# Differential attention with the values stationary, and its norm by a block matrix, in a one-layer hybrid decoder

## The chip, the cores and the metric

One core of a Trainium2 chip runs the whole layer as one program. Its engines work side by side, each through a list of instructions in order, and wait for each other by semaphores: TensorE (PE: matrix products, with PEld its weight loads), VectorE (DVE), ScalarE (ACT), GpSimd (POOL) and SyncE (SP, which starts DMAs here). The metric is the device time of one execution in microseconds.

## The reference

One layer on x of 256 x 1024: a SwiGLU, a mixer and another SwiGLU, each followed by a layer norm. The mixer runs three causal attentions of six heads with 64 columns each, and merges them with sigmoid gates:

```python
x = layer_norm(alpha*x + 0.5*swiglu(x, ...))
h = x @ w_in                      # q, k, v of the three branches, and gates
# MoBA: one block of 256 here, so causal softmax attention with ALiBi
# differential attention, per head:
p = softmax(s, axis=-1)           # s: two score maps, 32 columns each
w = p[:, :, 0] - lam * p[:, :, 1]
o = w @ v
o = o * rsqrt(mean(square(o), axis=-1) + 1e-5) * subln_g * (1 - lambda_init)
# stick-breaking attention: weights by sums of log-sigmoids
merged = sum(sigmoid(g_b + c_b) * (o_b @ w_br_b) for b in branches)
x = layer_norm(alpha*x + merged @ w_out)
x = layer_norm(alpha*x + 0.5*swiglu(x, ...))
```

## The kernel before

All products are exact to nearly float32: a weight chunk and an activation are each split into a high and a low part in float32r (`act_split`: ACT writes the high part, DVE the rest), and three products are summed. `Weights` streams chunks of 128 x 1024 through nine buffers; L106 (ACT) and L107 (DVE) are its split, L109 and L110 the same for the chunks that carry the sublayer norm's gain.

The order of all work is written out by the program while it is built. `MIX` lists the projections of q and k (`project`, which ends with L826 to L830: DVE and ACT take q and k out of their two banks), the gates (`gates`, whose banks are taken out by L868) and the branch products (`branch`, L890). `Pe` counts a modelled time as products are written, and pieces that were put off with `pe.later(delay, fn)` are written between two products once that model reaches their time. Each engine then works through what was written for it in just that order.

The heads go in pairs, first three stick-breaking ones, then three differential, then three MoBA. A pair passes through stages, one per slot, and a slot begins at the earliest 10 us (`PACE`) behind the one before, by the model. In a slot every pair under way takes its next stage, sorted by `KINDS`. A differential pair has four: `scores` (the products of q and k, then maxima on DVE in L616, exponentials on ACT in L622, and `combine`), `turn` (transposes of the weights, copied out as eT in L630), `pv` (values, then the norm), `turn_o` (transposes of o, split into oT). A MoBA pair has `scores` (with L616 and L622 too, and `norm` put off by 2 us: a reciprocal in L665 and four scalings in L668), `turn` and `valT`. The products with weights use four PSUM banks (`acc`), the attention four others (`att`); a bank is written again only after its readers are through, the oldest free one first.

```python
KINDS = ("sums", "turn_o", "pv", "turn", "valT", "scores")
def project(b, p):
    ...
    at = max(pe.t + 1.0, next_start[0])
    next_start[0] = at + PACE
    ...
    pe.later(at - pe.t, lambda: slot(attend[b](p, *res)))
```

Of the kernel before, what the change touches and what calls it, by code (L numbers as in the profile page):

```python
# [10 lines left out]
F32 = mybir.dt.float32  # L11
F32R = mybir.dt.float32r
AF = mybir.ActivationFunctionType
ALU = mybir.AluOpType
PSUM = bass.MemoryType.PSUM

P = 128
S = 256
# [4 lines left out]
HD = 64  # L23
BW = 384
NP = BW // P
EPS = 1e-5
# [27 lines left out]
T_M = 3.4  # L54
N_T = 4.5
M_N = 2.0
D_S = 2.5
E_BUFS = 6


class Weights:
# [129 lines left out]
def trunk(ctx: ExitStack, tc: tile.TileContext, start_d, x_d, ln_g, ln_b, gu_d, gun_d, down_d, v_d, qk_d, gate_d,  # L191
          b_gate, lam_d, subln_d, br_d, wo_d, out_d):
    nc = tc.nc
# [8 lines left out]
    small = ctx.enter_context(tc.tile_pool(name="small", bufs=4))  # L202
    acc = ctx.enter_context(tc.tile_pool(name="acc", bufs=4, space=PSUM))
    att = ctx.enter_context(tc.tile_pool(name="att", bufs=4, space=PSUM))
# [25 lines left out]
    pe = Pe(nc)  # L230
# [4 lines left out]
    def act_split(dst_h, dst_l, src):  # L235
        nc.scalar.activation(dst_h, src, AF.Copy)  # L236
        nc.vector.tensor_tensor(dst_l, src, dst_h.bitcast(F32), op=ALU.subtract)


    with ExitStack() as es:  # L240
        st = es.enter_context(tc.tile_pool(name="start", bufs=1))
        raws = []
        for k in range(KT):
            r = st.tile([P, S + 512], F32, name=f"sraw{k}")
# [12 lines left out]
        ident = const.tile([P, P], F32, name="ident")  # L257
        make_identity(nc, ident)
        first = []
        for k in range(KT):  # L260
# [3 lines left out]
            c = slice((k % 2) * 512, (k % 2) * 512 + 512)  # L264
# [19 lines left out]
    with ExitStack() as es:  # L284
        st = es.enter_context(tc.tile_pool(name="start2", bufs=1))
        mhalf = const.tile([P, 8], F32, name="mhalf")
# [37 lines left out]
    nlam = const.tile([P, 1], F32, name="nlam")  # L324
# [231 lines left out]
    with ExitStack() as es:  # L556
        mp = es.enter_context(tc.tile_pool(name="mp", bufs=1))
        qkp = es.enter_context(tc.tile_pool(name="qkp", bufs=3))
        ep = es.enter_context(tc.tile_pool(name="ep", bufs=E_BUFS))
        V = mp.tile([P, 2, 3 * BW], F32, name="V")  # L560
        oT = [mp.tile([P, NP, 2 * S], F32R, name=f"oT{b}") for b in range(3)]
# [26 lines left out]
        def vcol(b, h):  # L588
            return slice(b * BW + h * HD, b * BW + (h + 1) * HD)

        def scores(maps, qT, kT, row_q):


            st, mv = (qT, kT) if row_q else (kT, qT)
            for kind in range(2):
                for r0, n, ps in maps:
                    r, tp = slice(r0, r0 + n), (r0, 0)
                    if row_q and kind == 0:
                        out, a, b_ = ps[:, 0:P], slice(0, P), slice(0, P)
                    elif row_q:  # L600
                        out, a, b_ = ps[:, P:BW], slice(P, S), slice(0, S)
                    elif kind == 0:
                        out, a, b_ = ps[:, 0:S], slice(0, P), slice(0, S)
                    else:
                        out, a, b_ = ps[:, S:BW], slice(P, S), slice(P, S)
                    pe.mm(out, st[r, a], mv[r, b_], row_q or kind == 0, row_q, tile_position=tp, share=len(maps),
                          skip_group_check=not row_q)
# [3 lines left out]
        def exp_rows(maps):  # L611


            for ps, slope, e, nmx, _ in maps:
                for t, cs in enumerate(TILES):
                    nc.vector.tensor_tensor_reduce(e[:, cs], ps[:, cs], base[:, cs], -slope, 3e38, ALU.add, ALU.min,  # L616
                                                   accum_out=nmx[:, t:t + 1])
            W.quiet = False
            W.pump()
            for _, _, e, nmx, sm in maps:  # L620
                for t, cs in enumerate(TILES):
                    nc.scalar.activation(e[:, cs], e[:, cs], AF.Exp, bias=nmx[:, t:t + 1], scale=-1.0,  # L622
                                         accum_out=sm[:, t:t + 1])
# [9 lines left out]
        def values_T(b, p, eTs):  # L633

            po = att.tile([P, 512], F32, name="att")
            for kt, cs, ws in ((0, slice(0, S), slice(0, S)), (1, slice(P, S), slice(S, BW))):
                for r in range(2):
                    pe.mm(po[r * HD:(r + 1) * HD, cs], V[:, kt, vcol(b, 2 * p + r)], eTs[r][:, ws], kt == 0, kt == 1,
                          tile_position=(0, r * 64), share=2, skip_group_check=True)
            act_split(oT[b][:, p, 0:S], oT[b][:, p, S:2 * S], po[:, 0:S])  # L640
            pairs_done[b] += 1

        exps = [0]
        pairs_done = [0, 0, 0]
# [1 line left out]

        KINDS = ("sums", "turn_o", "pv", "turn", "valT", "scores")

        def moba_pair(p, qT, kT):
            sm = small.tile([P, 2, 2], F32, name="sm")
# [23 lines left out]
        def diff_pair(p, qT, kT):  # L676
            sm = small.tile([P, 2, 2, 2], F32, name="smd")
            nmx = small.tile([P, 2, 2, 2], F32, name="nmxd")
            ee, eTs, os_ = [], [], []

            def start():
                banks = [(acc if i < 2 else att).tile([P, 512], F32, name="acc" if i < 2 else "att")
                         for i in range(4)]
                scores([(i * 32, 32, banks[i]) for i in range(4)], qT, kT, True)
                ee.extend(ep.tile([P, BW], F32, name="e") for _ in range(4))
                exp_rows([(banks[i], SLOPES[2 * (2 * p + i // 2) + 1], ee[i], nmx[:, i % 2, i // 2, :],
                           sm[:, i % 2, i // 2, :]) for i in range(4)])
                exps[0] -= 1

                def combine(r):  # L690
                    c = small.tile([P, 2], F32, name="c")
                    nc.vector.reciprocal(c, sm[:, 1, r, :])
                    nc.vector.scalar_tensor_tensor(c, sm[:, 0, r, :], nlam, c, op0=ALU.mult, op1=ALU.mult)
                    e0, e1 = ee[2 * r], ee[2 * r + 1]
                    for t, cs in enumerate((slice(0, P), slice(P, BW))):
                        nc.vector.scalar_tensor_tensor(e0[:, cs], e1[:, cs], c[:, t:t + 1], e0[:, cs],
                                                       op0=ALU.mult, op1=ALU.add)
                for r in range(2):
                    combine(r)

            def pv():
                ps = att.tile([P, 512], F32, name="att")
                for r in range(2):
                    vc, eT = vcol(1, 2 * p + r), eTs[r]
                    o0, o1 = ps[:, r * HD:(r + 1) * HD], ps[:, P + r * HD:P + (r + 1) * HD]
                    pe.mm(o0, eT[:, 0:P], V[:, 0, vc], True, True)
                    pe.mm(o1, eT[:, P:S], V[:, 0, vc], True, False)
                    pe.mm(o1, eT[:, S:BW], V[:, 1, vc], False, True)
                rs = small.tile([P, 2, 2], F32, name="rsm")
                nc.vector.reciprocal(rs, sm[:, 0])  # L710
                o = ep.tile([P, S], F32, name="o", bufs=1)
                o4 = o.rearrange("p (t r c) -> p t r c", t=2, r=2)
                nc.vector.tensor_tensor(
                    o4, ps[:, 0:S].rearrange("p (t r c) -> p t r c", t=2, r=2),
                    rs.rearrange("p r t -> p t r").unsqueeze(3).to_broadcast([P, 2, 2, HD]), op=ALU.mult)
                sq = ep.tile([P, S], F32, name="s1", bufs=3)
                nc.vector.tensor_tensor(sq, o, o, op=ALU.mult)
                ms = small.tile([P, 4], F32, name="ms")
                nc.vector.tensor_reduce(ms, sq.rearrange("p (a c) -> p a c", c=HD), axis=mybir.AxisListType.X,
                                        op=ALU.add)  # L720
                nc.vector.tensor_scalar(ms, ms, 1.0 / HD, EPS, op0=ALU.mult, op1=ALU.add)
                nc.gpsimd.tensor_tensor(ms, ms, mhalf[:, 0:4], op=ALU.pow)
                os_.append(o)

                def scale():
                    nc.vector.tensor_tensor(
                        o4, o4, ms.rearrange("p (t r) -> p t r", t=2).unsqueeze(3).to_broadcast([P, 2, 2, HD]),
                        op=ALU.mult)
                pe.later(D_S, scale)

            def turn_o():
                ps = att.tile([P, 512], F32, name="att")
                for t in range(2):
                    pe.tr(ps[:, t * P:(t + 1) * P], os_[0][:, t * P:(t + 1) * P], ident)
                act_split(oT[1][:, p, 0:S], oT[1][:, p, S:2 * S], ps[:, 0:S])
                pairs_done[1] += 1

            return [{"scores": start},
                    {"turn": lambda: eTs.extend(turn_rows(e) for e in ee[::2])},
                    {"pv": pv},  # L740
                    {"turn_o": turn_o}]

        def stick_pair(p, qT, kT):
            zs, wts, split = [], [], []
# [50 lines left out]
        def slot(new=None):  # L795
# [3 lines left out]
            now = [pair.pop(0) for pair in under_way]  # L799
            for kind in KINDS:  # L800
                for stage in now:
# [172 lines left out]
```

## Time and profile before

| | us |
|---|---|
| median of three timed runs | 599.16 (598.97 to 599.27) |
| the profiled execution's own time | 598.51 |
| its span, first to last instruction | 596.8 |
| PE busy | 587.8 (98%) |
| DVE busy | 407.5 (68%) |
| ACT busy | 328.2 (55%) |
| granted clock of PE, mean | 0.995 |

A span is a little under the time of the execution. Matmuls are pipelined, so the lengths that the profile gives single ones overlap; what a piece of PE's work takes is read from its start to the start of the next piece. A float32 product stands as two records, one in float32r as one. Idle time of an engine that nobody waits for costs nothing.

### The profile page before, as it was taken

Reading aid. Unit: us, or ns where it says so; the run is one execution under the profiler, and the core shown is the slowest. Engines: PE = TensorE matmul, PEld = TensorE weight load, DVE = VectorE, ACT = ScalarE, POOL = GpSimd, SP = SyncE. Lnnn points to the kernel's source line nnn. Section 1 sums busy time; section 2 is a strip of 40 time slices with the busy share of each in tenths; the row PEclk is TensorE's granted clock in tenths of the full one; section 3 lists DMA queues with packets and bytes.
Section 4 is the critical chain, followed back from the end, with each engine's and each line's share of the span. In section 5 each row is a group of like instructions: output and inputs, shape, how many; then the busy total and the mean of one; then the engine's idle time right before and its main releaser. Section 6 shows DMA issues by size and latency. Waiting matters only on the chain.

```text
span 596.8 us, 8546 instructions
## 1 busy us (share of the span) xinstructions
PE 587.8 (98%) x3150; PEld 505.2 (85%) x3150; DVE 407.5 (68%) x655; ACT 328.2 (55%) x556; POOL 32.4 (5%) x71
## 2 busy tenths in 40 slices
PE   8999999999999999999999999999999999999995
PEld 7888888888888998888888878888898898888884
DVE  6889767674338746597977685889867667774217
ACT  5868656663312758596657654535665655654100
POOL 1610000000001002110001000001000000000001
PEclk9999999999999999999999999999999999999998
DMA  8999755666431576354547447256965565565001
GB/s 320 316 392 314 241 187 180 207 188 226 141 125 63 200 258 237 118 176 150 171 139 245 145 158 264 97 183 217 330 229 177 180 202 186 180 207 178 1 0 70
DMA packets 32538, 113.34 MB, mean 190 GB/s; under 512 B 3681, under 2 KB 4449, under 8 KB 32497
## 3 DMA queue, kind: packets, MB, share of 16 engines
q1 hardware_dynamic: 30672, 106.77, 53.2%
q0 software_dynamic: 1680, 5.83, 3.0%
q8 instruction: 24, 0.39, 0.3%
q10 hardware_dynamic: 144, 0.20, 0.1%
q14 instruction: 18, 0.14, 0.1%
HBM read 111.74 MB, written 1.05 MB: 189 GB/s over the span
## 4 chain that ended last, share of the span: by engine, by line
PE 97%; DMA 1%; DVE 1%; issue 0%; SPq 0%; ACT 0%; DVEq 0%
PE acc L182 91%; PE att L182 4%; PE att L186 2%; DMA sraw<-start 1%; DVE x L364 0%; DVE x L360 0%; ACT w L275 0%; DVE st L448 0%; DVE x L447 0%; SPq L249 0%; DVEq L968 0%; SPq L246 0%; DVE mv L353 0%
## 5 line engine op out<-in xcount | busy, mean ns | idle before, releaser
L107 DVE TENSOR_TENSOR w<-raw,w 128x1024 fp32r<-128x1024 f32 (+1 forms) x166 | 197.8, 1208 | 61.7 <-ACT w L106 60.8
L182 PE MATMUL acc<-xT,w 128*128 128x512 f32 (+1 forms) x1264 | 226.4, 337 | 0.0
L182 PEld LDWEIGHTS acc<-xT,w 128*128 128x128 f32 x1264 | 196.3, 190 | 26.6 <-issue 1.0
L106 ACT ACTIVATE w<-raw 128x1024 fp32r<-128x1024 f32 (+1 forms) x166 | 170.3, 1042 | 52.2 <-PE acc L182 44.0
L182 PE MATMUL acc<-w,xT 128*128 128x512 f32 (+1 forms) x576 | 128.1, 379 | 0.0
L182 PEld LDWEIGHTS acc<-w,xT 128*128 128x128 f32 x576 | 105.5, 188 | 18.6 <-issue 1.0
L182 PE MATMUL acc<-w,hT 128*128 128x512 f32 (+1 forms) x408 | 93.1, 383 | 0.0
L182 PEld LDWEIGHTS acc<-w,hT 128*128 128x128 f32 x408 | 75.2, 188 | 14.9
L475 ACT ACTIVATE lo<-acc 128x256 f32<-128x256 f32 x76 | 28.8, 384 | 57.3 <-PE acc L182 57.3
L477 DVE TENSOR_TENSOR gu<-acc,lo 128x256 f32<-128x256 f32 x76 | 31.6, 423 | 34.7 <-ACT lo L475 34.6
L182 PE MATMUL acc<-xT,wx 128*128 128x256 f32 (+1 forms) x240 | 46.1, 337 | 0.0
L107 DVE TENSOR_TENSOR wx<-raw,wx 128x1024 fp32r<-128x1024 f32 (+1 forms) x30 | 36.3, 1214 | 12.5 <-ACT wx L106 12.5
L182 PEld LDWEIGHTS acc<-xT,wx 128*128 128x128 f32 x240 | 37.5, 190 | 4.4
L106 ACT ACTIVATE wx<-raw 128x1024 fp32r<-128x1024 f32 (+1 forms) x30 | 31.3, 1047 | 11.3 <-PE acc L182 10.2
L354 ACT ACTIVATE rs<-mv 128x1 f32<-128x1 f32 x6 | 1.2, 204 | 59.6 <-DVE mv L353 59.6
L182 PE MATMUL acc<-wx,hT 128*128 128x512 f32 (+1 forms) x138 | 32.8, 380 | 0.0
L182 PEld LDWEIGHTS acc<-wx,hT 128*128 128x128 f32 x138 | 25.2, 188 | 4.9
L355 POOL TENSOR_TENSOR rs<-rs,mhalf 128x1 f32<-128x1 f32 x6 | 5.3, 892 | 407.9 <-ACT rs L354 407.9
L346 DVE SCALAR_TENSOR_TENSOR x<-x,acc 128x512 f32<-128x512 f32 x11 | 7.5, 683 | 27.4 <-PE acc L182 27.4
L182 PE MATMUL acc<-w,oT 128*128 128x512 f32 x108 | 25.7, 393 | 0.0
L182 PEld LDWEIGHTS acc<-w,oT 128*128 128x128 f32 x108 | 20.1, 188 | 4.4 <-issue 0.3
L236 ACT ACTIVATE hT<-gu 128x256 fp32r<-128x256 f32 x38 | 15.8, 417 | 11.5 <-DVE gu L482 11.5
(146 smaller groups left out, 412.9 us busy)
## 6 DMA issues: line engine op xcount, KB each, us to landing
raw<-gu SPq DMA_DIRECT2D x76, 512.0 KB, 4.8
raw<-down SPq DMA_DIRECT2D x44, 512.0 KB, 4.2
raw<-gates SPq DMA_DIRECT2D x24, 512.0 KB, 4.4
raw<-qk SPq DMA_DIRECT2D x18, 512.0 KB, 4.5
raw<-v SPq DMA_DIRECT2D x12, 384.0 KB, 3.0
raw<-w_out SPq DMA_DIRECT2D x8, 512.0 KB, 4.3
raw<-gun SPq DMA_DIRECT2D x8, 512.0 KB, 4.3
sraw<-start SPq DMA_DIRECT2D x7, 384.0 KB, 6.6
```

The costliest lines, as they stand in the source:

```text
L106: self.nc.scalar.activation(h[:, :n], raw[:, :n], AF.Copy)
L107: self.nc.vector.tensor_tensor(l[:, :n], raw[:, :n], hv[:, :n], op=ALU.subtract)
L182: self.nc.tensor.matmul(out, lhsT=lhsT, rhs=rhs, start=start, stop=stop, **kw)
L186: self.nc.tensor.transpose(out, in_, ident)
L236: nc.scalar.activation(dst_h, src, AF.Copy)
L346: nc.vector.scalar_tensor_tensor(xs, xs, ALPHA, ps[:, 0:n], op0=ALU.mult, op1=ALU.add)
L354: nc.scalar.activation(rs, mv[:, 1:2], AF.Copy, bias=EPS)
L355: nc.gpsimd.tensor_tensor(rs, rs, mhalf[:, 0:1], op=ALU.pow)
L475: nc.scalar.activation(lo, ps[:, S:2 * S], AF.Copy)
L477: nc.vector.tensor_tensor(v, ps[:, 0:S], lo, op=ALU.add)
```

## The change

The differential pairs keep the values stationary, as the other two branches do (`values_T`), so that o comes out with the head's columns on the partitions and needs no transposes. The first softmax is divided by its sum on ACT before the two are combined. The mean square over a head's 64 columns, now across partitions, is a product of a constant block matrix `mean64` with the split square of o (`rms`, L728 adds the epsilon and so empties the bank), one slot later. `finish`, put off by `R_F` = 2 us, works out the inverse square root as exp(-0.5 ln c), improves it by one Newton step, scales o with it and splits the result into oT. The pool of exponentials shrinks from six buffers to four.

```diff
-D_S = 2.5
-E_BUFS = 6
+R_F = 2.0
+E_BUFS = 4
...
+            if b == 1:
+                return po
             act_split(oT[b][:, p, 0:S], oT[b][:, p, S:2 * S], po[:, 0:S])
...
-        KINDS = ("sums", "turn_o", "pv", "turn", "valT", "scores")
+        KINDS = ("sums", "turn", "valT", "scores")
+
+        mean64 = ep.tile([P, P], F32R, name="mean64", bufs=1)
+        m32 = ep.tile([P, S], F32, name="s1", bufs=3)
+        nc.gpsimd.memset(m32, 0.0)
+        for r in range(2):
+            nc.gpsimd.memset(m32[r * HD:(r + 1) * HD, r * HD:(r + 1) * HD], 1.0 / HD)
+        nc.gpsimd.tensor_copy(mean64, m32[:, 0:P])
...
-                def combine(r):
-                    c = small.tile([P, 2], F32, name="c")
-                    nc.vector.reciprocal(c, sm[:, 1, r, :])
-                    nc.vector.scalar_tensor_tensor(c, sm[:, 0, r, :], nlam, c, op0=ALU.mult, op1=ALU.mult)
+                rs = small.tile([P, 2, 2, 2], F32, name="rsd")
+                nc.vector.reciprocal(rs, sm)
+                nc.vector.tensor_scalar(rs[:, 1], rs[:, 1], nlam, None, op0=ALU.mult)
+                for r in range(2):
                     e0, e1 = ee[2 * r], ee[2 * r + 1]
                     for t, cs in enumerate((slice(0, P), slice(P, BW))):
-                        nc.vector.scalar_tensor_tensor(e0[:, cs], e1[:, cs], c[:, t:t + 1], e0[:, cs],
+                        nc.scalar.activation(e0[:, cs], e0[:, cs], AF.Copy, scale=rs[:, 0, r, t:t + 1])
+                    for t, cs in enumerate((slice(0, P), slice(P, BW))):
+                        nc.vector.scalar_tensor_tensor(e0[:, cs], e1[:, cs], rs[:, 1, r, t:t + 1], e0[:, cs],
                                                        op0=ALU.mult, op1=ALU.add)
-                for r in range(2):
-                    combine(r)
-
-            def pv():
...
+            def values():
+                po = values_T(1, p, eTs)
+                o = ep.tile([P, S], F32, name="o", bufs=2)
+                nc.scalar.activation(o, po[:, 0:S], AF.Copy)
+                sq = ep.tile([P, S], F32, name="s1", bufs=3)
+                nc.vector.tensor_tensor(sq, po[:, 0:S], o, op=ALU.mult)
+                sp = ep.tile([P, 2 * S], F32R, name="sq", bufs=1)
+                act_split(sp[:, 0:S], sp[:, S:2 * S], sq)
+                os_.extend((o, sp))
+
+            def rms():
+                o, sp = os_
                 ps = att.tile([P, 512], F32, name="att")
-                for r in range(2):
-                    vc, eT = vcol(1, 2 * p + r), eTs[r]
-                    o0, o1 = ps[:, r * HD:(r + 1) * HD], ps[:, P + r * HD:P + (r + 1) * HD]
-                    pe.mm(o0, eT[:, 0:P], V[:, 0, vc], True, True)
-                    pe.mm(o1, eT[:, P:S], V[:, 0, vc], True, False)
-                    pe.mm(o1, eT[:, S:BW], V[:, 1, vc], False, True)
...
-                nc.gpsimd.tensor_tensor(ms, ms, mhalf[:, 0:4], op=ALU.pow)
...
-            def turn_o():
-                ps = att.tile([P, 512], F32, name="att")
-                for t in range(2):
-                    pe.tr(ps[:, t * P:(t + 1) * P], os_[0][:, t * P:(t + 1) * P], ident)
-                act_split(oT[1][:, p, 0:S], oT[1][:, p, S:2 * S], ps[:, 0:S])
-                pairs_done[1] += 1
+                for n in range(2):
+                    pe.mm(ps[:, 0:S], mean64, sp[:, n * S:(n + 1) * S], n == 0, n == 1)
+                c = ep.tile([P, S], F32, name="ms", bufs=1)
+                nc.vector.tensor_scalar(c, ps[:, 0:S], EPS, None, op0=ALU.add)
+
+                def finish():
+                    f = ep.tile([P, S], F32, name="s1", bufs=3)
+                    nc.scalar.activation(f, c, AF.Ln)
+                    nc.scalar.activation(f, f, AF.Exp, scale=-0.5)
+
+                    nc.vector.tensor_tensor(c, c, f, op=ALU.mult)
+                    nc.vector.tensor_tensor(c, c, f, op=ALU.mult)
+                    nc.vector.tensor_scalar(c, c, -0.5, 1.5, op0=ALU.mult, op1=ALU.add)
+                    nc.vector.tensor_tensor(o, o, f, op=ALU.mult)
+                    nc.vector.tensor_tensor(o, o, c, op=ALU.mult)
+                    act_split(oT[1][:, p, 0:S], oT[1][:, p, S:2 * S], o)
+                    pairs_done[1] += 1
+                pe.later(R_F, finish)
...
-                    {"pv": pv},
-                    {"turn_o": turn_o}]
+                    {"valT": values},
+                    {"sums": rms}]
```

Lines below this move by some six: L665 and L668 (the MoBA scalings) become L675 and L678, L826 to L830 become L832 to L836, L868 becomes L874, L890 becomes L896.

Three places show what it does to the order. The first is PE's slot D, the one in which the second MoBA pair's scores stand (128x256 of kT, qT). In the kernel before (ident,o are the transposes of o; V are the values, e the exponentials, ident the identity of a transpose):

```order
L182 MATMUL acc<-xT,w 128x512 x31
L186 MATMUL att<-ident,o 128x128 x2
L182 MATMUL att<-V,eT 128x64 x6
L186 MATMUL att<-ident,e 128x128 x6
L182 MATMUL att<-kT,qT 128x128 x2
L182 MATMUL att<-kT,qT 128x256 x2
L182 MATMUL acc<-xT,w 128x512
L182 MATMUL acc<-xT,w 128x256 x16
L182 MATMUL acc<-w,xT 128x512 x25
```

and in the changed one (sq is the split square, mean_2136 the block matrix):

```order
L182 MATMUL acc<-xT,w 128x512 x32
L182 MATMUL acc<-xT,w 128x256 x3
L182 MATMUL att<-sq,mean_2136 128x256 x2
L186 MATMUL att<-ident,e 128x128 x6
L182 MATMUL att<-eT,V 64x256 x2
L182 MATMUL att<-eT,V 64x128 x2
L182 MATMUL att<-kT,qT 128x128 x2
L182 MATMUL att<-kT,qT 128x256 x2
L182 MATMUL acc<-xT,w 128x256 x13
L182 MATMUL acc<-w,xT 128x512 x31
```

The transposes of o are gone, the value products stand behind the turn and have 256 columns, one wide and three narrow products of the projection have moved ahead of the slot, and six products of the gate ahead of the next one.

The second place is what follows the second MoBA pair's scores. DVE in the kernel before, from the last of that pair's maxima to its scalings (ms is the norm's factor, g_84 the gain):

```order
L616 ISA nmx 128x1
L726 TENSOR_TENSOR o<-o,ms 128x256
L827 SCALAR_TENSOR_TENSOR qT<-acc,qsc,s_3228 128x256
L830 TENSOR_TENSOR kT<-acc,s_3232 128x256
L110 SCALAR_TENSOR_TENSOR w<-raw,g_84,w 128x1024 x2
L665 RECIPROCAL rsm<-sm 128x4
L668 TENSOR_SCALAR e<-e,rsm 128x128
```

and in the changed kernel:

```order
L616 ISA nmx 128x1
L735 TENSOR_TENSOR ms<-ms,s_3217 128x256
L736 TENSOR_TENSOR ms<-ms,s_3217 128x256
L737 TENSOR_SCALAR ms<-ms 128x256
L738 TENSOR_TENSOR o<-o,s_3217 128x256
L739 TENSOR_TENSOR o<-o,ms 128x256
L237 TENSOR_TENSOR oT_1894<-o,oT_1894 128x256
L833 SCALAR_TENSOR_TENSOR qT<-acc,qsc,s_3239 128x256
L836 TENSOR_TENSOR kT<-acc,s_3243 128x256
L110 SCALAR_TENSOR_TENSOR w<-raw,g_84,w 128x1024 x2
L675 RECIPROCAL rsm<-sm 128x4
L678 TENSOR_SCALAR e<-e,rsm 128x128
```

One multiply has become five operations and a subtraction, between the maxima and the scalings. On ACT, at the same place, the kernel before has the last exponential and then:

```order
L622 ACTIVATE e,sm<-e,nmx 128x256
L826 ACTIVATE s_3228<-acc,qsc 128x256
L829 ACTIVATE s_3232<-acc 128x256
L109 ACTIVATE w<-raw,g_84 128x1024 x3
L236 ACTIVATE oT_1894<-att 128x256
```

and the changed one:

```order
L622 ACTIVATE e,sm<-e,nmx 128x256
L732 ACTIVATE s_3217<-ms 128x256
L733 ACTIVATE s_3217<-s_3217 128x256
L236 ACTIVATE oT_1894<-o 128x256
L832 ACTIVATE s_3239<-acc,qsc 128x256
L835 ACTIVATE s_3243<-acc 128x256
L109 ACTIVATE w<-raw,g_84 128x1024 x3
```

The logarithm, the exponential and the split of o, which waits for DVE's L739, stand ahead of the projection's evacuation.

The third place is DVE one slot later, from the weight split behind the third MoBA pair's maxima to the evacuation of the gate's two banks (bg is the gates' bias). The kernel before:

```order
L107 TENSOR_TENSOR w<-raw,w 128x1024
L665 RECIPROCAL rsm<-sm 128x4
L668 TENSOR_SCALAR e<-e,rsm 128x128
...
L668 TENSOR_SCALAR e<-e,rsm 128x256
L107 TENSOR_TENSOR w<-raw,w 128x1024
L868 TENSOR_TENSOR G<-acc,bg 128x512 x2
```

and the changed one:

```order
L107 TENSOR_TENSOR w<-raw,w 128x1024
L735 TENSOR_TENSOR ms<-ms,s_3349 128x256
...
L739 TENSOR_TENSOR o<-o,ms 128x256
L237 TENSOR_TENSOR oT_1894<-o,oT_1894 128x256
L107 TENSOR_TENSOR w<-raw,w 128x1024
L675 RECIPROCAL rsm<-sm 128x4
...
L678 TENSOR_SCALAR e<-e,rsm 128x256
L874 TENSOR_TENSOR G<-acc,bg 128x512 x2
```

The five operations and the subtraction of the third differential pair stand ahead of it, and with them all that follows.

## Rows read from the trace of the kernel before

**Rows 1.** The page, busy time of each engine: us (share of the span) x instructions

```profile
PE 587.8 (98%) x3150; PEld 505.2 (85%) x3150; DVE 407.5 (68%) x655; ACT 328.2 (55%) x556; POOL 32.4 (5%) x71
```

**Rows 2.** All waits of PE in the run: who waited <- for whom: us, times, longest

```profile
PE att L256 <- DVE warm L252: 1.1, 1, 1.1
PE att L182 <- ACT w L275: 0.6, 1, 0.6
```

**Rows 3.** PE's timeline, 285 to 332 us: start, length, line, out<-in, shape, count

```profile
285.55 1.45 PE L182 MATMUL att<-V,eT 128*128 128x64 f32 x12
286.83 0.83 PE L186 MATMUL att<-ident,e 128*128 128x128 f32 x6
...
301.90 0.38 PE L186 MATMUL att<-ident,o 128*128 128x128 f32 x2
302.12 1.45 PE L182 MATMUL att<-V,eT 128*128 128x64 f32 x12
...
305.02 8.04 PE L182 MATMUL acc<-xT,w 128*128 128x256 f32 x37
312.90 0.38 PE L186 MATMUL att<-ident,o 128*128 128x128 f32 x2
...
316.01 2.41 PE L182 MATMUL acc<-xT,w 128*128 128x512 f32 x17
...
323.96 0.38 PE L186 MATMUL att<-ident,o 128*128 128x128 f32 x2
324.18 0.82 PE L186 MATMUL att<-ident,e 128*128 128x128 f32 x6
324.92 0.87 PE L182 MATMUL att<-eT,V 128*64 128x256 f32 x8
325.73 0.93 PE L182 MATMUL att<-kT,qT 64*128 64x128 f32 x8
326.58 5.51 PE L182 MATMUL acc<-w,xT 128*128 128x512 f32 x23
331.93 5.61 PE L182 MATMUL acc<-w,oT 128*128 128x512 f32 x24
```

**Rows 4.** Timeline of DVE and ACT beside it (first piece ahead of 285.55)

```profile
281.62 0.19 ACT L622 ACTIVATION_READ_ACCUMULATOR e<-e,nmxd 128x1 f32 x1
...
316.11 0.29 DVE L616 CUSTOM_DVE_ANT_0 e<-att,base 128x128 f32<-128x128 f32 x1
...
316.45 0.40 ACT L622 ACTIVATE e<-e,nmx 128x128 f32<-128x128 f32 x1 [0.64 <-DVE nmx L616]
...
318.22 0.46 ACT L826 ACTIVATE s<-acc,qsc 128x256 f32<-128x256 f32 x1
...
318.91 3.45 ACT L109 ACTIVATE w<-raw,g 128x1024 fp32r<-128x1024 f32 x3
...
320.09 2.48 DVE L110 SCALAR_TENSOR_TENSOR w<-raw,g,w 128x1024 fp32r<-128x1024 f32 x2 [0.57 <-ACT w L109]
...
322.70 1.01 DVE L668 TENSOR_SCALAR e<-e,rsm 128x128 f32<-128x128 f32 x4
...
331.65 1.28 DVE L868 TENSOR_TENSOR G<-acc,bg 128x512 f32<-128x512 f32 x2
```

**Rows 5.** Groups by line and shape: xcount | busy us, mean ns of one | idle before

```profile
L182 PE MATMUL acc<-xT,w 128*128 128x256 f32 x632 | 82.2, 284 | 0.0
...
L481 ACT ACTIVATE gu<-gu 128x256 f32<-128x256 f32 x38 | 15.5, 408 | 0.3 <-DVE gu L477 0.3
...
L668 DVE TENSOR_SCALAR e<-e,rsm 128x256 f32<-128x256 f32 x6 | 2.1, 349 | 0.0
...
L717 DVE TENSOR_TENSOR s<-o 128x256 f32<-128x256 f32 x3 | 1.3, 425 | 0.1
```

**Rows 6.** Stretches at the run's end: busy us of PE, PEld, DVE, ACT, POOL; granted clock (PEclk); DMA

```profile
588.00:590.00 2.00, 1.51 (x13) 1.31 (x11) 1.01 (x3) 0.00 (x0) 0.00 (x0) 1.00 0.00 0
590.00:592.00 2.00, 0.00 (x0) 0.00 (x0) 1.92 (x4) 0.20 (x1) 0.88 (x1) 0.85 0.00 0
```

More of the change, by code (lines that the diff above doesn't have):

```diff
@@ L697, in combine @@
                                                        op0=ALU.mult, op1=ALU.add)
-                for r in range(2):
-                    combine(r)
-            def pv():
-                ps = att.tile([P, 512], F32, name="att")
-                for r in range(2):
-                    vc, eT = vcol(1, 2 * p + r), eTs[r]
-                    o0, o1 = ps[:, r * HD:(r + 1) * HD], ps[:, P + r * HD:P + (r + 1) * HD]
-                    pe.mm(o0, eT[:, 0:P], V[:, 0, vc], True, True)
-                    pe.mm(o1, eT[:, P:S], V[:, 0, vc], True, False)
-                    pe.mm(o1, eT[:, S:BW], V[:, 1, vc], False, True)
[L709 to L721, printed above, removed]
-                nc.gpsimd.tensor_tensor(ms, ms, mhalf[:, 0:4], op=ALU.pow)
[L723 to L729, printed above, removed]
```

## The prediction

> **What bounds the kernel now.** I read the page's busy times first: TensorE (PE) is busy 587.8 of 596.8 us [rows 1]. Then the waits of PE: they come to 1.7 us in all, both in the first 8 us [rows 2]. So for the whole rest of the run, the mixer included, PE never waits for a result. Time can come off only by giving PE less to do, and it is lost as soon as PE must wait for VectorE (DVE) or ScalarE (ACT). Last I read PE's timeline through the attention slots, where its work stands in one unbroken row [rows 3], and beside it DVE and ACT in the same stretch [rows 4], to see how early each result is there.
>
> I call the slots by where they begin in the trace of before: B 285.55, C 301.90, D 312.90, E 323.96, F 337.37. The reader is to see in [rows 3] that work follows work without a gap, and in [rows 4] that at E it is already close: the four scalings of the second MoBA pair run from 322.70 to 323.71, and PE's transposes of the same rows start at 324.18 [rows 3, 4]. That cover is 0.5 us, and it is on this chain that the change puts work.
>
> **The change part by part.**
>
> *PE.* Removed per pair: the value products with 128 stationary and 64 moving columns, 285.55 to 286.83 = 1.28 us, and the two transposes of o, 301.90 to 302.12 = 0.22. Added: the products with the values stationary, 324.92 to 325.73 = 0.81 for the same shape in the MoBA branch [rows 3], and two fp32r products of 256 columns. Those I price by the group of that shape, 82.2 us over 632 = 0.13 each, 0.26 for two; the bound above is a lone product's 0.284 each, 0.57 [rows 5]. Per pair 1.28 + 0.22 - 0.81 - 0.26 = 0.43 us, over three pairs **1.3 us less PE work** (0.4 at the upper bound).
>
> *Edits that cost nothing.* The combination of the softmaxes becomes a reciprocal (0.2), four ACT scalings (at most 0.41 each, 1.6) and a last DVE operation (0.42): ready 2.2 us after the exponentials. At its tightest, ahead of B, these end at 281.8 [rows 4], so 284.0 against transposes at 285.55: covered by 1.5 us, and what it is late it costs if that cover goes. Six e buffers become four: each is written again only by maxima that follow, on PE too, the transposes that read it, so no wait is added. The four POOL operations that build the block matrix come at the start of the mixer, tens of microseconds before slot C needs it. The weight splits (L106, L107) that get delayed by a few microseconds serve products 10 us and more later: the pair ending at 322.57 (L110) feeds the second branch product, and the first one only begins at 331.93 [rows 3, 4].
>
> *What is moved onto the chain.* The norm of each pair was one small POOL step and one DVE multiply. Now it is Ln and Exp on ACT, five DVE operations, and a split (ACT, then DVE) from SBUF, and it stands in both queues behind the exponentials of the pair that started in the same slot. On ACT it is ahead of the next projection's evacuation (L832, L835) and of the weight splits; on DVE it is ahead of the MoBA scalings (L678) that PE's next transposes wait for. ACT is held while it waits for DVE's five, and DVE while it waits for ACT's half of the split. Prices, from the nearest rows: Ln, Exp 0.41 each (the SiLU of that shape, 0.408); a DVE operation on 128x256 0.425, a tensor_scalar 0.349; with 0.46 from one dependent operation to the next this makes 0.85 for Ln and Exp, 2.1 for the five, 0.4 + 0.4 for the split [rows 5]. Together 3.8. No row has these operations, so bounds: each like the tensor_scalar, 0.35, or like an ACT operation that also reads a scale, 0.46 (318.22, [rows 4]); with nine operations that is 3.2 to 4.2. I take 3.8, since the 0.41 to 0.425 are rows of the same shape, and keep both ends.
>
> *Slot by slot.* Times on PE are those of before minus what is saved so far.
>
> C starts at 301.4 and its value products end at 303.2. On ACT follow a copy of o (0.4), after DVE's square (0.42) the split (0.3 until the next starts), two weight splits (1.9) and the exponentials of MoBA pair 1 (1.77, as 316.45 to 318.22 [rows 4]): 308.2. Then Ln, Exp 0.85, the five 2.1, ACT's and DVE's split 0.8: 312.0. The reciprocal and four scalings take 0.2 and 0.92: ready at 312.6 for the first of the two rows, 313.1 for both.
>
> D: C's work is 0.26 + 0.74 + 0.81 + 0.85 = 2.66 instead of 3.12, the stretch behind it 7.88 (305.02 to 312.90, [rows 3]) and 0.6 more, because the order puts one 512- and three 256-column products ahead of D. So D starts at 312.55, its transposes at 312.8: just in time. After them DVE does the projection's q and k (0.75, to 313.8), two weight splits (2.3, a little under the 2.48 of the scaled ones [rows 4]; to 316.1), the EPS add (0.35), the square (0.42), waits for ACT's half of the split (0.42) and does its own (0.34). The maxima of MoBA pair 2 start at **317.6**; now they start at 316.11 [rows 4]. (The bank for PE's scores frees behind two ACT splits here, 0.5 us late; this only uses up part of the wait that follows.)
>
> E: from the maxima's start, now: exponentials 316.45 to 318.22, q and k evacuated, the scaled splits L109 from 318.91, L110 320.09 to 322.57, scalings from 322.70 [rows 4]. After: maxima 317.6, exponentials to 319.7, Ln and Exp to 320.5, the five to 322.6, ACT's split to 323.0, the two evacuations on ACT (0.7, as 318.22 to 318.91) to 323.7, first L109 (3.45/3 = 1.15) to 324.85, two L110 (2.4) to 327.2, reciprocal and the first row's scalings (0.2 + 0.5): **327.9**. PE wants them at: D 312.55 + 2.66, then 7.95 (316.01 to 323.96) with three 256-column products fewer and six 512-column ones more (+1.0), then the mean-square product: 324.4. **PE waits about 3.5 us.**
>
> F: turn, values and scores of E end at 327.9 + 2.4 = 330.3 on PE. MoBA pair 3: maxima 330.4, exponentials to 332.6, Ln and Exp 333.45, the five 335.5, ACT's split 336.0, a weight split on ACT and DVE (2.1, a little under the scaled ones' 1.15 + 1.24) to 338.1, reciprocal and scalings 339.2, and only then the evacuation of the gate banks (L868, 1.28 for two): the first is free at **339.9**. Of PE's four accumulation banks the branch product's third group needs this one. PE gets there after 17 products of the gate (17 x 0.233, from 326.58 to 331.93 for 23) and two groups of nine (18 x 0.234): 330.3 + 4.0 + 4.2 = 338.5. A second wait, 1.4 us. Now the same group starts at 331.93 + 4.2 = 336.1, and from there PE's work is the same.
>
> **Sum.** 339.9 - 336.1 = **+3.8 us**, or -1.3 of PE work and +5.1 of waits. The profiled execution took 598.51 us with a span of 596.8, so 602.3; the three timed runs have a median of 599.16, 0.65 above it, so **602.9 us**. What a measurement can tell from no change is about 0.2%, 1.2 us.
>
> **The rivals.**
> - *The cover holds, only the saving is left: 597.8.* One mechanism decides: the scalings at E must be ready at 324.4 instead of 327.9. For it: every link is from rows, but none is of the new operations. Against it: even with the norm's whole chain at nothing (3.8 us off) they would just be ready, for the maxima are 1.5 us late before that. It decides from there.
> - *Half the waits: near 599 to 601.4.* The wait at E is as worked out, but the gate's banks come free early, or the new operations overlap better than dependent ones in the rows. 601.4 with the first alone; within 0.2% of 599.16 if 3.8 of the 5.1 us vanish.
> - *The clock falls in the wait: 605.3.* At the run's end PE works up to 589.5 (1.51 us busy of the two from 588) at a granted clock of 1.00; over the two us from 590, with no product at all, it is 0.85 [rows 6]. [...] What it does in a wait of 3.5 us in the midst of work no row shows. [...]
> - *The combination is late at B*, since ACT now scales four rows first. It would take over 1 us of error; it would cost what it is late, less than 1 us.
>
> **How the numbers follow.** The forecast's chain, 602.9, with plus or minus 1.4 for some twenty links at 0.05 to 0.1 us: 0.55 (601.5 to 604.3). The clock's case 0.18. Half the waits, but over 600.4: 0.08; within 1.2 us of now 0.07; the cover holds 0.12. So faster 0.12, same 0.07, slower 0.81. The range 599.4 to 606.0 leaves out the cover's case and the lower half of "same" below, about 0.16, and a deeper fall of the clock above, 0.03. Slower is nearly all of it, so the range of the likeliest one alone is the 601.5 to 604.3 above.
>
> **What would show it.** The saving: the value products of the differential pairs 0.81 us long at B, C and D, no transposes of o, two 256-column products in front of C, D and E. The chain: in PE's waits a wait of some 3.5 us in front of E's transposes, ended by DVE's scaling (L678), and one of 1.4 in front of the branch product, ended by DVE's gate evacuation (L874); ACT idle before L236 for DVE's L739. The clock: granted clock under 1.0 between 325 and 340. It is wrong if PE shows no waits there (then 597.8), if Ln and Exp come with table loads, or if the chain's five DVE operations take well under 2 us.

## The result: slower by 1.4%, twice what was forecast

The changed kernel took 607.18 us (607.13 to 607.27), the kernel before, beside it, 599.07: a ratio of 1.0139, interval 1.0127 to 1.0152. The forecast was 602.9 with a range up to 606.0. So the sign was right, and 4.3 us are missing from the sum.

The profiled execution has a span of 605.5 us where the kernel before had 596.8. The page's busy times of the changed kernel, which answer to [rows 1]:

```profile
PE 592.9 (98%) x3138; PEld 504.7 (83%) x3138; DVE 410.1 (68%) x655; ACT 336.3 (56%) x580; POOL 30.0 (5%) x72
```

And all waits of PE, which answer to [rows 2]:

```profile
PE att L186 <- DVE e L678: 3.0, 1, 3.0
PE acc L182 <- DVE G L874: 1.2, 1, 1.2
PE att L256 <- DVE warm L252: 1.1, 1, 1.1
```

Both forecast waits are there, each ended by the line that was named: 3.0 us ahead of E's transposes (forecast 3.5) and 1.2 us ahead of the branch product (forecast 1.4). PE's own timeline shows the work of slots C, D and E and what came behind the first wait; it answers to [rows 3].

```profile
302.74 0.40 PE L182 MATMUL att<-sq,mean 128*128 128x256 f32 x2
...
305.38 8.61 PE L182 MATMUL acc<-xT,w 128*128 128x256 f32 x41
...
315.80 1.30 PE L182 MATMUL att<-kT,qT 64*128 64x128 f32 x8
317.03 1.81 PE L182 MATMUL acc<-xT,w 128*128 128x256 f32 x13
...
325.74 0.40 PE L182 MATMUL att<-sq,mean 128*128 128x256 f32 x2
329.09 1.44 PE L186 MATMUL att<-ident,e 128*128 128x128 f32 x6 [2.96 <-DVE e L678]
330.46 1.55 PE L182 MATMUL att<-eT,V 128*64 128x256 f32 x8
331.94 1.32 PE L182 MATMUL att<-kT,qT 64*128 64x128 f32 x8
333.19 4.15 PE L182 MATMUL acc<-w,xT 128*128 128x512 f32 x17
...
342.74 3.05 PE L182 MATMUL acc<-w,oT 128*128 128x512 f32 x12 [1.21 <-DVE G L874]
```

Slot C takes 2.64 us (302.74 to 305.38) instead of the 3.12 of [rows 3]: the saving is there, 0.48 a pair. But at E the turn, the values and the scores take 4.10 us (329.09 to 333.19) where the kernel before took 2.40 (324.18 to 326.58), with the same instructions. The same view for ACT and DVE shows the chain that held PE; it answers to [rows 4].

```profile
321.01 0.40 ACT L732 ACTIVATE s<-ms 128x256 f32<-128x256 f32 x1
...
321.89 0.43 DVE L735 TENSOR_TENSOR ms<-ms,s 128x256 f32<-128x256 f32 x1 [1.79 <-ACT s L733]
...
323.47 0.42 DVE L739 TENSOR_TENSOR o<-o,ms 128x256 f32<-128x256 f32 x1
323.93 0.42 ACT L236 ACTIVATE oT<-o 128x256 fp32r<-128x256 f32 x1 [2.07 <-DVE o L739]
...
324.38 0.43 DVE L237 TENSOR_TENSOR oT<-o,oT 128x256 fp32r<-128x256 f32 x1 [0.48 <-ACT oT L236]
...
326.06 2.48 DVE L110 SCALAR_TENSOR_TENSOR w<-raw,g,w 128x1024 fp32r<-128x1024 f32 x2 [0.49 <-ACT w L109]
...
328.66 1.01 DVE L678 TENSOR_SCALAR e<-e,rsm 128x128 f32<-128x128 f32 x4
```

From the logarithm at 321.01 to the end of the split at 324.81 it is 3.8 us, the price that was taken. ACT stands idle for 2.07 us of it, until DVE's L739 is done. The stretches of the run around it (PE, PEld, DVE, ACT and POOL busy, then the granted clock) show why E's work is slow:

```profile
326.00:328.00 2.00, 0.14 (x2) 0.00 (x0) 1.94 (x2) 2.00 (x3) 0.00 (x0) 1.00 0.00 0
328.00:330.00 2.00, 0.91 (x5) 0.86 (x6) 1.97 (x7) 0.17 (x2) 0.00 (x0) 0.85 0.82 260
330.00:332.00 2.00, 2.00 (x13) 0.96 (x11) 1.20 (x2) 0.91 (x2) 0.00 (x0) 0.50 0.88 262
332.00:334.00 2.00, 2.00 (x14) 1.53 (x13) 1.13 (x6) 1.70 (x4) 0.00 (x0) 0.80 0.73 225
334.00:336.00 2.00, 2.00 (x10) 1.68 (x9) 1.64 (x5) 1.97 (x10) 0.00 (x0) 1.00 0.11 43
```

PE has nothing to do from 326.1 to 329.1. Up to 328, in the midst of this wait, the granted clock is still 1.00; over 328 to 330 it is 0.85, over 330 to 332, where PE is busy throughout, 0.50, and it is back at 1.00 from 334 on.

Yet not all that is lost lies here. Slot A, the one ahead of B, begins 1.3 us later than before (275.68 instead of 274.35), and 1.4 us more come in the last 60 us, where the program is unchanged. Both lags build up in the two down projections (the last product of each SwiGLU), whose stationary operand is `hT`. PE's timeline of the first one:

```profile
127.67 8.54 PE L182 MATMUL acc<-w,hT 128*128 128x512 f32 x36
136.04 2.94 PE L182 MATMUL acc<-wx,hT 128*128 128x512 f32 x12
```

That is 0.2325 us from one start to the next. In the kernel before the same 36 products go from 127.84 to 136.00, 0.2267 each. The groups of the changed kernel (count | busy us, mean ns of one), to be set beside those of the first experiment below:

```profile
L182 PE MATMUL acc<-w,hT 128*128 128x512 f32 x384 | 92.1, 395 | 0.0
...
L182 PE MATMUL acc<-wx,hT 128*128 128x512 f32 x126 | 31.7, 394 | 0.0
...
L182 PE MATMUL acc<-w,oT 128*128 128x512 f32 x108 | 26.2, 397 | 1.2 <-DVE G L874 1.2
```

From the traces, then: work saved -1.4 us, the waits +4.2, D's scores +0.5 (1.23 us to 317.03 instead of 0.85, and their start 0.15 late: their banks come free late, as forecast), E's slow work +1.7, and the products on `hT` and `oT` +3.4 (worked out below). That is 8.4 of the 8.7 us by which the span grew; 0.3 are not accounted for.

### The profile page after: what moved, and what is told of

Read it like the earlier page. It is cut to its first block, busy times and chain, and to the rows that moved or that the text cites. A ratio compares the mean times of both kernels' runs of the same rounds, so it can differ in the third digit from the quotient of the medians.

```text
span 605.5 us, 8547 instructions
## 1 busy us (share of the span) xinstructions
PE 592.9 (98%) x3138; PEld 504.7 (83%) x3138; DVE 410.1 (68%) x655; ACT 336.3 (56%) x580; POOL 30.0 (5%) x72
## 4 chain that ended last, share of the span: by engine, by line
PE 93%; DVE 3%; ACT 2%; issue 1%; DVEq 0%; ACTq 0%
PE acc L182 86%; PE att L182 4%; PE att L186 2%; ACT e L622 1%; DVE w L107 1%; PE att L256 1%; ACT w L106 0%; DVE e L678 0%; DVE w L110 0%; DVE ms L735 0%; DVE ms L736 0%; DVE o L739 0%; ACT s L733 0%; DVE x L364 0%; ACT w L109 0%
## 5 line engine op out<-in xcount | busy, mean ns | idle before, releaser
L182 PE MATMUL acc<-w,hT 128*128 128x512 f32 (+1 forms) x408 | 95.3, 388 | 0.0
```

Of the source, the lines that this page charges most:

```text
L182: self.nc.tensor.matmul(out, lhsT=lhsT, rhs=rhs, start=start, stop=stop, **kw)
```

## The experiments

They ran in three groups, each beside the kernel before, which took 598.67 us (`place_back`, `before_moved`, `fill`, `spread`), 598.65 (`spread_low`, `norm_first`, `no_newton`, `place_bench`) and 598.81 (`place_bench2`, `moved_256`). Ratios are to the kernel before of the same group. `fill`, `spread`, `norm_first` and `no_newton` also have the added line of `place_back`, which is left out of their cuts. A kernel with an added line has its lines one higher than the changed kernel.

**The place of hT (`place_back`).** The change takes two kinds of small tiles (`c`, `ms`) out of a pool and puts one (`rsd`) in, four buffers of 32 bytes each, so that all that stands behind them in SBUF, `hT`, the values and `oT` too, begins 128 bytes lower. This kernel gives the 128 bytes back.

```diff
     small = ctx.enter_context(tc.tile_pool(name="small", bufs=4))
+    small.tile([P, 32], F32, name="pad", bufs=1)
```

> The changed kernel with 128 unused bytes per partition behind the small tiles, so that hT, the values and oT stand at the addresses of the kernel before (hT at 173632 instead of 173504). Order and work are unchanged. Theory, placement: in the changed kernel the products that read hT start every 0.232 us and in the one before every 0.227, and this comes from the address; the lag of 1.2 us that builds up over the first down projection, 1.4 over the second and some 0.6 over the branch products go, so about 604.0 us, with the starts 0.227 apart again. Rival: the address has nothing to do with it (another execution, other traffic), so 607.2 as before. Both waits of PE stay, about 3.0 and 1.2 us.

604.49 us, a ratio of 1.0096 (1.0082 to 1.0110): 2.7 us come back with nothing else changed, or 2.3 if each kernel is measured against the kernel before beside it. The same groups:

```profile
L182 PE MATMUL acc<-w,hT 128*128 128x512 f32 x384 | 89.9, 389 | 0.0
...
L182 PE MATMUL acc<-wx,hT 128*128 128x512 f32 x126 | 31.0, 389 | 0.0
...
L182 PE MATMUL acc<-w,oT 128*128 128x512 f32 x108 | 25.7, 393 | 0.6 <-DVE G L875 0.6
```

The 618 products take 2.2 + 0.7 + 0.5 = 3.4 us less, 5.5 ns each; from start to start those on `hT` are 0.227 us apart again (the first 36 go from 127.82 to 135.98). The time falls by less than 3.4, and the trace shows one loss on the other side: the wait ahead of E is 2.96 us as before, but the clock stays down longer behind it. E's work takes 4.50 us here, and the granted clock over 332 to 334 is still 0.56, where the changed kernel had 0.80:

```profile
327.77 1.51 PE L186 MATMUL att<-ident,e 128*128 128x128 f32 x6 [2.96 <-DVE e L679]
...
332.27 4.85 PE L182 MATMUL acc<-w,xT 128*128 128x512 f32 x17
```

```profile
332.00:334.00 2.00, 2.00 (x7) 1.39 (x6) 1.62 (x9) 1.43 (x8) 0.00 (x0) 0.56 0.29 115
```

So the same wait does not have one price.

**The same for the kernel before (`before_moved`).**

```diff
-                ms = small.tile([P, 4], F32, name="ms")
+                ms = ep.tile([P, 4], F32, name="ms", bufs=4)
```

> The kernel before, with only its four 16-byte ms tiles moved to the pool behind, so that hT, the values and oT come 128 bytes lower, to the changed kernel's address 173504. Theory, placement: about 599.1 + 3.2 = 602.3 us, PE's products on hT 0.232 apart, no waits. Rival: 599.1 as before.

602.20 us, a ratio of 1.0060 (1.0047 to 1.0074), with no wait of PE that was not there before. So 3.5 us hang on the address alone, in a kernel that is otherwise the old one.

**The wait filled with work (`fill`).**

```diff
+                if p == NP - 1:
+                    for n in 12 * (0, 1):
+                        nc.tensor.matmul(ps[:, 0:S], lhsT=mean64, rhs=sp[:, n * S:(n + 1) * S], start=n == 0, stop=n == 1)
                 c = ep.tile([P, S], F32, name="ms", bufs=1)
```

> place_back, with the two mean-square products of the third differential pair written 13 times over instead of once (24 more products of 256 columns, 2.9 us, each pair starting its bank anew), so that PE works through most of the wait in front of the second MoBA pair's transposes. Theory, the clock: the slow transposes, values and scores behind that wait (4.1 us instead of 2.4) are the clock granted at half after idling; with the wait filled the granted clock stays 1.00, these take 2.4 us, and the run is 1.7 us shorter than place_back, 602.3. Rival: they are slow for another reason (traffic to memory, the banks), so the same as place_back, 604.0.

603.00 us, a ratio of 1.0073 (1.0060 to 1.0085), 1.5 less than `place_back`. PE's timeline and one stretch:

```profile
325.06 3.04 PE L730 MATMUL att<-sq,mean 128*128 128x256 f32 x24
328.18 1.07 PE L186 MATMUL att<-ident,e 128*128 128x128 f32 x6
...
330.83 4.19 PE L182 MATMUL acc<-w,xT 128*128 128x512 f32 x17
...
340.42 3.02 PE L182 MATMUL acc<-w,oT 128*128 128x512 f32 x12 [1.31 <-DVE G L878]
```

```profile
330.00:332.00 2.00, 2.00 (x15) 1.47 (x14) 1.77 (x9) 1.90 (x5) 0.00 (x0) 1.00 0.87 248
```

E's work begins 0.4 us later than in `place_back` (328.18, there 327.77), as slot C already does (301.83, there 301.41), but then takes 2.65 us to 330.83 instead of 4.50, and the granted clock is 1.00 from 322 to 336. So the slow stretch was the clock, and the cause was the idle time: useless products in the wait make the run shorter. The last 0.25 us to the 2.40 of the kernel before are not the clock's, which stays at 1.00 here; they are there too in `no_newton` below (2.65 us behind a wait of 0.4). Of the 1.7 us that E's work lost in the changed kernel the clock's part is thus about 1.45.

**The norm taken apart (`spread`).** The logarithm and the exponential go on ACT ahead of the next pair's softmax, the five DVE operations behind that pair's maxima, the split later by itself.

```diff
-M_N = 2.0
-R_F = 2.0
+M_N = 1.0
+R_F = 3.0
...
-        KINDS = ("sums", "turn", "valT", "scores")
+        KINDS = ("sums", "turn", "valT", "ln", "scores", "fin")
...
-                    {"sums": rms}]
+                    {"sums": rms, "ln": ln, "fin": fin}]
```

> place_back, with the norm of a differential pair taken apart: its logarithm and exponential on ACT ahead of the next pair's softmax exponentials, its five DVE operations behind that pair's maxima, where DVE waits for the exponentials anyway, and its split 3 us later; and the MoBA scalings 1 us behind the scores instead of 2. Theory, the place in the queues: both waits go, the clock stays up and 1.3 us of PE work are saved, so 599.1 - 1.3 = 597.8, 597.4 to 598.6. Rival: ACT and DVE simply have too much to do between two slots, wherever it stands; a wait of 1 to 3 us remains ahead of slot E or of the gates' banks, 599.5 to 603.

597.42 us, a ratio of 0.9977 (0.9969 to 0.9986): faster than the kernel before, by 1.25 us where 1.3 were expected. That is little, but its slowest execution (598.12) lies under the fastest of the kernel before (598.24). PE has no wait left but that of the first microseconds. ACT and DVE in slot D:

```profile
315.78 0.40 ACT L735 ACTIVATE s<-ms 128x256 f32<-128x256 f32 x1
...
317.35 0.42 DVE L741 TENSOR_TENSOR ms<-ms,s 128x256 f32<-128x256 f32 x1
...
318.93 0.43 DVE L745 TENSOR_TENSOR o<-o,ms 128x256 f32<-128x256 f32 x1
...
319.48 1.01 DVE L679 TENSOR_SCALAR e<-e,rsm 128x128 f32<-128x128 f32 x4
```

The five operations (317.35 to 319.36) lie behind the maxima, where DVE in the changed kernel waited for ACT (1.79 us ahead of L735), and the scalings begin at 319.48, 4.4 us before PE's transposes at 323.89. The edit does two things, the scalings earlier and the norm in pieces. `norm_first` below has the first without the second; the second alone was not run.

**`spread` at the low address (`spread_low`).** The line with the unused bytes is taken out.

> spread without the 128 unused bytes, so hT, the values and oT at the changed kernel's addresses. Theory: the placement costs here what it cost the kernel before, 3.5 us, so 597.4 + 3.5 = 600.9 us, slower than the kernel before although nothing waits. Rival: it costs less where PE has no other loss, 598 to 599.5.

601.03 us, a ratio of 1.0039 (1.0025 to 1.0052), 3.6 us over `spread`. With the low address the better order would have been read as a loss.

**Only the order of two pieces (`norm_first`).** `M_N` = 1 and `R_F` = 4, the norm in one piece.

> place_back with two numbers changed: the MoBA scalings 1 us behind the scores instead of 2, the norm of the differential pairs, in one piece, 4 us behind its products instead of 2, so that it stands behind the scalings. Theory, both queues: the wait ahead of E's transposes goes, but on ACT the split that waits for the five DVE operations, and a weight split behind it, now stand ahead of the copies of eT, so PE waits some 3 us ahead of E's value products instead; the same as place_back, 603.5 to 605. Rival, only the scalings' place counts: no wait at E, 598 to 600.

601.35 us, a ratio of 1.0042 (1.0029 to 1.0054), between theory and rival and 3.9 us over `spread`. The waits, and ACT at E:

```profile
PE att L182 <- ACT eT L631: 1.7, 2, 1.1
...
PE acc L182 <- DVE G L875: 1.0, 1, 1.0
```

```profile
325.95 0.42 ACT L237 ACTIVATE oT<-o 128x256 fp32r<-128x256 f32 x1 [2.85 <-DVE o L740]
...
327.31 0.85 ACT L631 ACTIVATE eT<-att 128x384 f32<-128x384 f32 x2
```

The wait ahead of the transposes is gone, and the hold on ACT (2.85 us for DVE's L740) and the late copies of eT (L631 at 327.31) are as worked out. But they did not hold the values, which use the eT of the slot before; they held the scores, whose banks the copies set free, for 1.1 us at E and 0.5 at D. The place I named was wrong, and so was the size.

**Four operations fewer (`no_newton`).** The inverse square root is left as exp(-0.5 ln c) gives it.

```diff
-                    nc.vector.tensor_tensor(c, c, f, op=ALU.mult)
-                    nc.vector.tensor_tensor(c, c, f, op=ALU.mult)
-                    nc.vector.tensor_scalar(c, c, -0.5, 1.5, op0=ALU.mult, op1=ALU.add)
                     nc.vector.tensor_tensor(o, o, f, op=ALU.mult)
-                    nc.vector.tensor_tensor(o, o, c, op=ALU.mult)
```

> place_back without the Newton step of the norm, that is one DVE operation instead of five (the inverse square root is as the tables give it, not improved). Theory, the length of the chain: four operations 0.44 us apart, 1.75 us, come off the wait at E, 2.96 to 1.2 us, and the wait ahead of the gates' banks goes; if the clock then stays up, 604.5 - 1.75 - 1.5 - 0.6 = 600.6, if it still falls 602.1. Rival: ACT's queue holds the chain anyway, the wait stays near 3 us and the time near 604.5.

597.99 us, a ratio of 0.9990 (0.9981 to 0.9998). The one wait that is left at E:

```profile
PE att L186 <- DVE e L679: 0.4, 1, 0.4
```

0.4 us, not 1.2: the chain is shorter in the slot before as well, so the maxima that start E's chain come at 316.38 instead of 317.58. I had counted the four operations once. Behind this wait E's work takes 2.65 us (324.99 to 327.64), and the run's mean granted clock is 0.998, as in `spread`, where PE has no such wait.

**What the address is measured against (`place_bench`, `place_bench2`, `moved_256`).** Both benches run products of constants on moving tiles at stepped addresses, one execution each. "64 over 256" means that an address leaves 64 when it is divided by 256.

> Products alone, no layer: 24 products of 512 columns of constants in float32r on each of 17 moving tiles, whose addresses are 23104 + 2080 i, so that 64 + 32 i is left over 512 (hT stands at 64 over 512 in the kernel before, at 448 in the changed one); then 24 products of 256 columns with each of eight stationary tiles, 576 bytes apart. The output is not the layer's. Theory, the place within 512 bytes decides: starts 0.227 us apart on the first tile and the last but one (64 over 512), 0.232 on the 13th (448 over 512), and the row shows which of the others are slow. Rival: the place counts in another way (a larger stride, or against the weights' address), then the 13th tile is like the first.

From start to start of a group, over 24: 0.2275 us on the ninth tile (320 over 512, like 64 over 256), 0.2279 on the last, the 17th (64 over 512; the expectation calls it the last but one), 0.2296 on the third and 11th (128 over 256), 0.233 to 0.234 on all others, the 13th (448 over 512) among them. The first tile's group cannot be told from the products that ran ahead of it on the same tile. So the pattern repeats every 256 bytes, not 512, and the theory was wrong in that. The stationary tile stands at 64 over 256 too. The groups of 256 columns took 0.117 to 0.120 us a product, in no order that I can read.

> Products of constants alone again (the output is not the layer's): 32 products of 512 columns on each of nine moving tiles, 32 bytes further over 256 from one to the next (64, 96, ..., 224, 0, 32, 64), first with stationary tiles at 64 over 256, as in the kernel, then with others at 192 over 256. In the first of these runs only moving tiles at 64 over 256 were fast, those at 128 half as much. Theory, the relation between the two operands: with the stationary tiles 128 bytes further the fast moving tile is the fifth, at 192, instead of the first and last, at 64. Rival: the moving address alone, so the first and last are fast in both halves.

Here ma is at 64 over 256, me at 192; w, the stationary tile, at 64, u at 192. PE's timeline, 32 products to a group:

```profile
14.98 7.45 PE L214 MATMUL acc<-ma,w 128*128 128x512 f32 x32
22.27 7.63 PE L214 MATMUL acc<-mb,w 128*128 128x512 f32 x32
...
44.55 7.63 PE L214 MATMUL acc<-me,w 128*128 128x512 f32 x32
52.01 7.65 PE L214 MATMUL acc<-mf,w 128*128 128x512 f32 x32
...
89.21 7.59 PE L214 MATMUL acc<-ma,u 128*128 128x512 f32 x32
96.63 7.65 PE L214 MATMUL acc<-mb,u 128*128 128x512 f32 x32
...
119.06 7.44 PE L214 MATMUL acc<-me,u 128*128 128x512 f32 x32
126.34 7.63 PE L214 MATMUL acc<-mf,u 128*128 128x512 f32 x32
```

With w, ma takes 7.29 us to the next start (0.2278 each) and me 7.46 (0.2331); with u, me takes 7.28 (0.2275) and ma 7.42 (0.2319). The fast place moves with the stationary operand.

> The kernel before with 256 unused bytes behind the small tiles, so hT, the values and oT stand 256 bytes higher (hT at 173888, again 64 over 256). Theory, the address counts over 256: no change, 598.7 us, PE's products on hT 0.227 apart. Rival, the old place was a lucky one: 3.5 us slower, 602.2.

598.59 us, a ratio of 0.9998 (0.9989 to 1.0007).

## Why the prediction was wrong, and where it was right

**The slots.** What the prediction works out slot by slot holds where its assumptions do. In `place_back`, which has the addresses it assumed: slot C at 301.41 (forecast 301.4), D at 312.51 (312.55), the second pair's maxima at 317.58 (317.6), the second L110 done at 327.21 (327.2), PE's transposes at 327.77 (327.9). The wait there is 3.0 instead of 3.5, because PE is through 0.4 later (324.81, forecast 324.4), after D's late banks, which the forecast had named and set off against it, and the transposes can start 0.1 earlier. The 3.8 us for the norm are 3.8, the saving of 0.43 a pair is 0.48. The logarithm and the exponential came without table loads of their own: the changed kernel has five in the run, of 1.28 us each, as the kernel before. In the run with neither a slow clock nor a moved tile, `fill`, the gate's bank lets PE go on at 340.42 (339.9), and the time is 603.0 where the sum said 602.9 (4.3 us over the kernel before beside it, where the sum said 3.8). The edits that were put at nothing cost nothing: before C no wait appears, so the rival of a late combination did not come about. Two slips in the sum are small: the waits that it names add up to 3.5 + 1.4 = 4.9, not 5.1, and it prices the products on `oT` at 5.61 / 24 = 0.234 us by their length, where from start to start they take (337.37 - 331.93) / 24 = 0.227.

**The step that failed: "from there PE's work is the same".** The instructions behind the branch product are the same, and those ahead of the mixer too, but the sum took the same time for them. It had no term for where the tiles come to lie once the small pool shrinks, which costs 3.5 us (`before_moved`) of the 4.3 that are missing: 602.9 + 3.5 = 606.4 is already over the range's 606.0.

**The step that was weighed wrongly: the clock.** The rival had a chance of 0.18 and is what happened: behind the 3.0 us wait the granted clock is 0.50 (330 to 332). The 2.4 us that its 605.3 adds to the forecast no run shows; E's work lost 1.7 in the changed kernel and 2.1 in `place_back` (0.25 of each without the clock), and the run 1.5 (`place_back` less `fill`). For the changed kernel itself no run takes the clock's part out. In `norm_first`, with waits of 1.1 and 1.0 us, the clock stayed at 1.00 (328 to 332 and 338 to 340).

**The other rivals.** That the cover would hold missed by 3.0 us in this order, but `spread` shows what it is worth: 1.25 us with the same operations in other places. Half the waits: they came almost whole, 4.2 of the 4.9 that were named.

The sum with both missing terms would be 602.9 + 3.5 + 1.5 = 607.9, 0.7 above the 607.2 measured.

## What to carry to other kernels

A side effect of a change can weigh more than the change (the address cost 3.6 us in `spread_low`, where the order of `spread` gained 1.25): when small buffers are added or dropped, compare the addresses of the large tiles, and the time per product of work that the change does not touch, before reading the result. Where PE is busy throughout, work moved to ACT and DVE should be cut into pieces that lie where those queues wait anyway, not put in one piece ahead of what PE needs next (597.42 us in `spread`, 604.49 in `place_back`). A wait of PE can cost more than its length: here the granted clock fell to 0.50 for products behind the 3.0 us wait, while it was 1.00 behind the changed kernel's wait of 1.2 us (342 to 346) and behind those of 1.1 and 1.0 us in `norm_first`.

## What the runs showed of the hardware

The time of the float32r products with 512 moving columns followed, in these runs, how the two operands lie to each other in SBUF: 0.227 to 0.228 us each when the moving one begins at the same place within 256 bytes as the stationary one (the kernel before, `place_bench`, `place_bench2`), 0.229 to 0.230 when it begins 64 bytes further (both benches), 0.232 to 0.234 at the other places tried, in steps of 32 bytes (both benches, and 0.2325 in the changed kernel). `place_bench2` shows that it is the relation and not an address by itself (ma 0.2278 with w and 0.2319 with u, me 0.2331 and 0.2275), and `moved_256` that a step of 256 bytes is free (598.59 us, the kernel before 598.81). In the kernel a weight chunk moves and `hT` or `oT` is stationary. From hT's address and the sizes of the tiles ahead of it, the weight chunks begin at 64 over 256; `hT` begins there too in the kernel before, and at 192 in the changed one. Why the place counts no run tells. In the first down projection it counts for 2.6% (0.2325 us from start to start in the changed kernel, 0.2267 in the one before).
